# A two-layer encoder trunk on one core: norm factor and offset behind the transpose, with edits to the first k, the scores, the loads and the gate half

## The chip, the core and the metric

The kernel runs on one core of a Trainium2 chip. A core has a matmul engine (PE, with its weight loads, PEld), a vector engine (DVE), a scalar engine (ACT), GpSimd (POOL) and a sync engine (SP) that issues the DMAs. Each engine works through its own queue in order. SBUF is the memory on the core, with 128 partitions; PSUM is where PE writes, in 8 banks of 128 x 512 fp32 values. The metric is the device time of one execution in microseconds (us). A profiled execution also has a span: the time from its first to its last instruction.

## The reference

The input is 256 frames of width 2048, in fp32. Two layers follow each other, and each has a token mixer and a gated MLP, both closed by a layer norm over the residual:

```python
for i in range(DEPTH):                       # DEPTH = 2
    if i % 2 == 0:
        m = gmlp_mixer(x, gm_w_in, gm_ln_g, gm_ln_b, gm_w_s, gm_b_s, gm_w_out)
    else:
        m = mla_mixer(x, mla_w_in, ...)
    x = layer_norm(ALPHA * x + m, ln_mix_g[i], ln_mix_b[i])
    f = conv_ffn(x, ffn_w_up[i], ffn_conv_w[i], ffn_conv_b[i], ffn_w_down[i])
    x = layer_norm(ALPHA * x + f, ln_ffn_g[i], ln_ffn_b[i])
```

- The gMLP mixer computes gelu(x @ w_in), 2048 to 2 x 6144, and splits it into u and v (v is the gate half). v gets a layer norm and a masked 128 x 128 mixing over positions, multiplies u, and goes through w_out, 6144 to 2048.
- The MLA mixer is latent attention: low-rank latents of 512 for queries and for keys with values, 16 heads, a rotary part of 64, a chunk-causal mask.
- conv_ffn is an up projection to 2 x 5504, a causal width-3 convolution over positions, silu(g) * a, and a down projection.
- layer_norm subtracts the mean, divides by the root of the variance plus 1e-5, multiplies by a factor g and adds an offset b, both 2048 wide.

## The kernel before

**Products in three parts.** Each fp32 operand is split into a high part, rounded to the fp32r format of PE, and the rest: ACT casts the high part, DVE subtracts it. A product is then high x high, low x high and high x low, three matmuls. The activations live as xhl tiles with high and low side by side. The weights are streamed from HBM in chunks of 128 x 2048 values (1 MB) by the class Feed: `_load` (L75) issues the DMA on SP, `_split` (L89) does the cast and the subtraction, and `next` (L137) gives a stage its chunk and runs two splits and two loads ahead, more at the end of a down projection.

**Seven instead of eight.** For some pairs of k (two 128-row slices of the weights, two blocks of 128 frames, two 512-wide columns, thus eight products), the kernel takes Strassen's form with seven (`seven`, L344). Such a chunk needs sums of the weights (`_seven`, L113: four more tiles and the adds on DVE) and four combinations of the activations (`combine`, L204), and its partial results go into four more PSUM banks (OWN) beside the usual four (DIRECT); `rest` (L354) puts them together. V_SEVEN says which pairs of the gate half do so in each of its six groups, BACK_SEVEN which k of the down projections.

**The stages in order.** v: six groups of eight chunks, 1024 columns each; `stats` (L567) collects the sums for v's norm. u: twelve groups of 512 columns, each followed by `gate` (L628). Then the down projection `down` (L392) in two halves of 1024 columns, the norm, and the MLP: 22 groups of up projection with `pair` (L682) and again `down`. Layer 1 is the attention (latents, queries, keys, values, scores, output) and the same MLP.

**The class Norm.** `piece` (L527) adds a result to the residual and takes statistics; `start` (L535) makes mean and reciprocal root; `scale` (L541) normalises 128 x 512 values of the residual in place; `put` (L549) transposes them on PE into a PSUM bank and splits them into the xhl tile of the next stage. `prep` (L514) loads factor and offset rows, broadcast over the partitions, towards the end of the down projection. `boundary` (L453) interleaves all that by hand with the last matmuls of the down projection and the first group of the next stage: three chunks of the last columns are kept back (SKEW), so that PE has work while the first 128 frames are normalised.

**First k.** `Sums.quad` (L373) splits four k's of the down projection's input at once into a tile of the pool "big"; `Sums.make` (L383) builds the combinations of a seven.

**Order and buffers.** A planner turns the program into one queue for each engine. It takes the instruction that stands first in the program among those it expects to be ready, so an instruction may move ahead of others that wait. Tiles of one tag share buffers: "big" has 22 of 128 x 2048 fp32 values, for weight chunks, residual, xhl, stage results and the norms' rows alike; "t1" and "t2" are small work tiles, 8 and 6 of them. A tile waits until a buffer of its tag is free.

Of the kernel before, what the change touches and what calls it, by code (L numbers as in the profile page):

```python
# [15 lines left out]
P = 128  # L16
# [32 lines left out]
V_PAIRS = [[0, 1, 2, 3, 4, 5, 6, 7]] + [[2, 0, 1, 4, 3, 5, 6, 7]] * 5  # L49
V_SEVEN = [()] + [(2, 3)] * 5  # L50
# [15 lines left out]
class Feed:  # L66
# [8 lines left out]
    def _load(self):  # L75
# [13 lines left out]
    def _split(self):  # L89
# [9 lines left out]
        step = 512 if i == 0 else cols if kind == "wide" else 1024 if cols == 2048 else cols // 2  # L99
# [45 lines left out]
def trunk(ctx: ExitStack, tc: tile.TileContext, x, xT, gm_in, gm_wout, ffn_up, ffn_dn,  # L145
# [56 lines left out]
    xc, xraw, xc_room = {}, [], [slot([P, 2, 8 * P], "xc0", F32R)]  # L202
# [163 lines left out]
    class Sums:  # L366
# [3 lines left out]
        def __init__(self, src, tag):  # L370
            self.src, self.tag, self.rooms, self.got, self.quads = src, tag, [], {}, {}

        def quad(self, q, n_k):  # L373
# [7 lines left out]
            self.quads[q] = t  # L381

# [9 lines left out]
    def down(n_k, src, tag, ln, sums, skew=SKEW):  # L392
# [5 lines left out]
        for hf, units in enumerate(halves(n_k)):  # L398
# [5 lines left out]
            for i, u in enumerate(units):  # L404
# [8 lines left out]
                a = [[x_parts(quads, k, b) for k in u] for b in range(2)]  # L413
# [84 lines left out]
    class Norm:  # L498
# [15 lines left out]
        def prep(self):  # L514
# [4 lines left out]
            nc.sync.dma_start(self.b, ln_rows[2 * i + 1 : 2 * i + 2, :].to_broadcast([P, D]))  # L519

# [20 lines left out]
        def scale(self, b, f):  # L541
            c = slice(f * 512, (f + 1) * 512)
            r = self.res[b][:, c]
            nc.vector.scalar_tensor_tensor(r, r, self.mu, self.g[:, c], ALU.subtract, ALU.mult)
            nc.vector.scalar_tensor_tensor(r, r, self.rs, self.b[:, c], ALU.mult, ALU.add)
            if self.last:
                nc.sync.dma_start(out[b * P : (b + 1) * P, c], r)

        def put(self, b, f):  # L549
# [7 lines left out]
            t3 = t.rearrange("p (j c) -> p j c", j=4)  # L557
            hi = self.new[f][:, :, b * P : (b + 1) * P]
            nc.scalar.copy(hi, t3)
            nc.vector.tensor_tensor(self.new[f][:, :, S + b * P : S + (b + 1) * P], t3, hi.bitcast(F32), ALU.subtract)  # L560
# [4 lines left out]
    vst = st.tile([P, 2, 12, 6], F32, tag="vst", name="vst", bufs=1)  # L565

    def stats(gi):  # L567
        for b in range(2):
            for f in range(2):
                nc.vector.bn_stats(vst[:, b, 2 * gi + f, :], v[gi][:, b, f * 512 : (f + 1) * 512])  # L570
# [525 lines left out]
```

## Time and profile before

| | us |
|---|---|
| median of 3 runs | 2514.16 |
| lowest and highest run | 2513.23, 2514.31 |
| profiled execution, its own time | 2514.31 |
| its span, first to last instruction | 2512.5 |
| PE busy | 2488.9 (99%) |
| DVE busy | 1833.0 (73%) |
| ACT busy | 1317.0 (52%) |

A row of the profile names line, engine, operation, and the tiles written and read (out<-in). Where a helper issues an instruction, the line is the helper's: all matmuls stand at L162. Waits are listed as waiter, releaser, us in total, times, longest. A stretch row has length, busy time and count of each engine, the granted share of the PE clock, the mean share of the DMA engines and GB/s. In a timeline row the first two numbers are start and duration in us; the bracket tells how long the engine had been idle and what ended that.

### The profile page before, as it was taken

Reading aid. Unit: us, or ns where it says so; the run is one execution under the profiler, and the core shown is the slowest. Engines: PE = TensorE matmul, PEld = TensorE weight load, DVE = VectorE, ACT = ScalarE, POOL = GpSimd, SP = SyncE. Lnnn points to the kernel's source line nnn. Section 1 sums busy time; section 2 is a strip of 40 time slices with the busy share of each in tenths; the row PEclk is TensorE's granted clock in tenths of the full one; section 3 lists DMA queues with packets and bytes.
Section 4 is the critical chain, followed back from the end, with each engine's and each line's share of the span. In section 5 each row is a group of like instructions: output and inputs, shape, how many; then the busy total and the mean of one; then the engine's idle time right before and its main releaser. Section 6 shows DMA issues by size and latency. Waiting matters only on the chain.

```text
span 2512.5 us, 32375 instructions
## 1 busy us (share of the span) xinstructions
PE 2488.9 (99%) x13081; PEld 2140.5 (85%) x13081; DVE 1833.0 (73%) x2411; ACT 1317.0 (52%) x1689; POOL 2.9 (0%) x17
## 2 busy tenths in 40 slices
PE   9999999999999999999999999999999999999998
PEld 7888888888887888888888888988888888888886
DVE  7877766678787767666777897766686677668797
ACT  5555544445464545554655564565365455546553
POOL 0000000000000000000000000000000000000000
PEclk9999999999999999999999999999999999999999
DMA  7555544556566545555546674444454455544654
GB/s 292 201 184 211 191 170 166 177 192 206 189 207 252 190 179 201 184 184 181 189 151 201 217 268 159 152 150 178 177 214 176 167 197 186 183 168 169 212 206 167
DMA packets 86021, 480.18 MB, mean 191 GB/s; under 512 B 7664, under 2 KB 8304, under 8 KB 46064
## 3 DMA queue, kind: packets, MB, share of 16 engines
q1 hardware_dynamic: 85872, 478.13, 53.4%
q8 instruction: 102, 1.67, 0.3%
q14 instruction: 47, 0.39, 0.0%
HBM read 476.00 MB, written 2.10 MB: 190 GB/s over the span
## 4 chain that ended last, share of the span: by engine, by line
PE 96%; DVE 2%; ACT 1%; DMA 1%; issue 0%; SPq 0%; DVEq 0%; ACTq 0%
PE up L162 35%; PE u L162 10%; PE dn_q L162 9%; PE dn_p L162 6%; PE v_q L162 5%; PE wo_q L162 5%; PE mo L162 3%; PE dn_e L162 3%; PE wo_p L162 3%; PE v_p L162 3%; PE v_e L162 2%; PE wo_e L162 2%; PE upf L162 2%; PE mkv L162 1%; PE qn L162 1%; PE kn L162 1%
## 5 line engine op out<-in xcount | busy, mean ns | idle before, releaser
L103 DVE TENSOR_TENSOR wl<-raw,wh 128x1024 fp32r<-128x1024 f32 (+3 forms) x667 | 940.9, 1434 | 226.4 <-ACT wh L102 166.8
L102 ACT CAST wh<-raw 128x1024 fp32r<-128x1024 f32 (+3 forms) x667 | 796.1, 1223 | 364.7 <-DVE wl L103 125.3
L162 PE MATMUL up<-xhl,wh 128*128 128x512 f32 x2624 | 610.7, 390 | 0.0
L162 PEld LDWEIGHTS up<-xhl,wh 128*128 128x128 f32 x2624 | 487.4, 188 | 97.8
L162 PEld LDWEIGHTS up<-xhl,wl 128*128 128x128 f32 x2624 | 325.8, 192 | 6.4
L162 PE MATMUL up<-xhl,wl 128*128 128x256 f32 x2624 | 328.1, 283 | 0.0
L162 PE MATMUL u<-xhl,wh 128*128 128x512 f32 x768 | 183.3, 392 | 0.6 <-DVE h_u L309 0.5
L162 PEld LDWEIGHTS u<-xhl,wh 128*128 128x128 f32 x768 | 141.5, 188 | 30.5 <-PE s L162 2.2
L110 ACT CAST th<-ts 128x1536 fp32r<-128x1536 f32 x80 | 83.2, 1053 | 93.5 <-DVE ts L117 80.7
L111 DVE TENSOR_TENSOR tl<-ts,th 128x1536 fp32r<-128x1536 f32 x80 | 95.0, 1219 | 4.9 <-ACT th L110 2.6
L162 PEld LDWEIGHTS u<-xhl,wl 128*128 128x128 f32 x768 | 95.3, 192 | 1.9
L162 PE MATMUL u<-xhl,wl 128*128 128x256 f32 x768 | 95.9, 283 | 0.0
L162 PE MATMUL v_q<-wh,xhl 128*128 128x512 f32 x304 | 94.0, 391 | 1.3 <-ACT wh L102 1.3
L162 PE MATMUL wo_q<-wh,woa 128*128 128x512 f32 x304 | 94.0, 390 | 0.0
L110 ACT CAST wh<-raw 128x1536 fp32r<-128x1536 f32 x40 | 59.3, 1482 | 50.1 <-DMA raw<-in_ffn_dn_dram 19.6
L162 PE MATMUL dn_q<-wh,dn1a 128*128 128x512 f32 x264 | 82.5, 392 | 2.0 <-DVE dn1a L380 2.0
L162 PE MATMUL dn_q<-wh,dn0a 128*128 128x512 f32 x264 | 82.0, 390 | 2.0 <-DVE dn0a L380 2.0
L162 PE MATMUL mo<-wh,oT 128*128 128x512 f32 x256 | 82.9, 404 | 0.0
L309 DVE TENSOR_TENSOR h_1a<-up,lo_1a 128x256 f32<-128x256 f32 x41 | 17.2, 420 | 75.4 <-ACT lo_1a L307 75.3
L309 DVE TENSOR_TENSOR h_0a<-up,lo_0a 128x256 f32<-128x256 f32 x41 | 17.2, 420 | 74.8 <-ACT lo_0a L307 74.6
L111 DVE TENSOR_TENSOR wl<-raw,wh 128x1536 fp32r<-128x1536 f32 x40 | 70.1, 1751 | 2.1 <-PE dn_q L162 2.1
L162 PEld LDWEIGHTS v_q<-wh,xhl 128*128 128x128 f32 x304 | 56.9, 188 | 13.8 <-ACT wh L102 2.0
(440 smaller groups left out, 3805.8 us busy)
## 6 DMA issues: line engine op xcount, KB each, us to landing
raw<-in_ffn_up_dram SPq DMA_DIRECT2D x172, 1024.0 KB, 4.7
raw<-in_gm_in_dram SPq DMA_DIRECT2D x95, 1024.0 KB, 4.8
raw<-in_ffn_dn_dram SPq DMA_DIRECT2D x84, 1024.0 KB, 5.3
raw<-in_gm_wout_dram SPq DMA_DIRECT2D x48, 1024.0 KB, 5.5
raw<-in_ml_out_dram SPq DMA_DIRECT2D x16, 1024.0 KB, 4.8
raw<-in_ml_b_dram SPq DMA_DIRECT2D x14, 1024.0 KB, 4.8
raw<-in_ml_kv_dram SPq DMA_DIRECT2D x5, 864.0 KB, 4.6
lng<-in_ln_rows_dram SPq DMA_DIRECT2D x4, 1024.0 KB, 7.9
```

The lines of the kernel that those rows point to most:

```text
L102: self.nc.scalar.copy(hi[:, c], raw[:, c])
L103: self.nc.vector.tensor_tensor(lo[:, c], raw[:, c], hi[:, c].bitcast(F32), ALU.subtract)
L110: self.nc.scalar.copy(hi, raw)
L111: self.nc.vector.tensor_tensor(lo, raw, hi.bitcast(F32), ALU.subtract)
L162: nc.tensor.matmul(o, l, r, start=start, stop=stop, skip_group_check=True)
L309: nc.vector.tensor_tensor(h, acc[:, 0:S], lo, ALU.add)
```

## The change

- **Norms.** In all norms but the last, `scale` only subtracts the mean and multiplies by the reciprocal root. `put` applies factor and offset behind the transpose, where they are one value for each partition: four ACT instructions of 128 x 128 with a column of `lncol` as scale and another as bias, into a work tile, which is then split. `lncol` holds all norms' factors and offsets as columns: the rows are loaded once as 128 x 128 values and transposed once on PE. The residual itself gets factor and offset in the next stage, by `restore`, from broadcast rows that are loaded there.
- **First k.** The first four k's of a down projection are split one by one into "t2" tiles (`first`); two combinations instead of four are made in the stage before, the others in the down projection.
- **Scores.** Three `attend_a` and two `attend_b` stand one step earlier between the products of the values.
- **Loads.** Chunks 1 and 2 are loaded and split in halves; the constants and the rotary tables are loaded behind the first group of v.
- **Gate half.** Three of eight chunks in five groups are made by seven products, where there were two, in another order and with another order of banks; v's sums come from the accumulators of ACT (gelu for the sum, a Square for the squares about a first mean), and DVE adds the partial results straight from PSUM.

```diff
-V_PAIRS = [[0, 1, 2, 3, 4, 5, 6, 7]] + [[2, 0, 1, 4, 3, 5, 6, 7]] * 5
-V_SEVEN = [()] + [(2, 3)] * 5
+V_PAIRS = [[0, 1, 2, 3, 4, 5, 6, 7]] + [[0, 2, 1, 5, 3, 6, 4, 7]] * 5
+V_SEVEN = [()] + [(2, 3, 4)] * 5
...
         else:
+            if self.loaded in (1, 2):
+                step = 1024
             for o in range(0, cols, step):
...
-        step = 512 if i == 0 else cols if kind == "wide" else 1024 if cols == 2048 else cols // 2
+        step = 512 if i == 0 else cols if kind == "wide" and i > 2 else 1024 if cols == 2048 else cols // 2
...
-    xc, xraw, xc_room = {}, [], [slot([P, 2, 8 * P], "xc0", F32R)]
+    xc, xraw, xc_room = {}, [], [slot([P, 2, 8 * P], f"xc{i}", F32R) for i in range(2)]
...
-    nc.sync.dma_start(cst, consts)
...
-    nc.sync.dma_start(rope_sb, ropes)
+    lncol = cpool.tile([P, P], F32, name="lncol")
...
+        def first(self):
+            for k in range(4):
+                x = self.src[0][:, k, :]
+                t = tp.tile([P, 512], F32R, tag="t2", name=f"{self.tag}f{k}", bufs=6)
+                nc.scalar.copy(t[:, 0:S], x)
+                nc.vector.tensor_tensor(t[:, S : 2 * S], x, t[:, 0:S].bitcast(F32), ALU.subtract)
+                self.parts[k] = t
+            self.quads[0] = None
...
-        def prep(self):
+        def rows(self):
             i = self.idx
             self.g = slot([P, D], f"lng{i}")
...
+        def prep(self):
+            if self.last:
+                self.rows()
+
+        def restore(self, b, f):
+            c = slice(f * 512, (f + 1) * 512)
+            r = self.res[b][:, c]
+            nc.vector.tensor_tensor(r, r, self.g[:, c], ALU.mult)
+            nc.vector.tensor_tensor(r, r, self.b[:, c], ALU.add)
...
             r = self.res[b][:, c]
+            if not self.last:
+                nc.vector.tensor_scalar(r, r, self.mu, self.rs, op0=ALU.subtract, op1=ALU.mult)
+                return
             nc.vector.scalar_tensor_tensor(r, r, self.mu, self.g[:, c], ALU.subtract, ALU.mult)
             nc.vector.scalar_tensor_tensor(r, r, self.rs, self.b[:, c], ALU.mult, ALU.add)
...
-            t3 = t.rearrange("p (j c) -> p j c", j=4)
+            y = tp.tile([P, 4, P], F32, tag="t2", name=f"lny{i}_{b}_{f}", bufs=6)
+            for j in range(4):
+                g, o = 32 * i + 4 * f + j, 32 * i + 16 + 4 * f + j
+                nc.scalar.activation(y[:, j], t[:, j * P : (j + 1) * P], AF.Identity, bias=lncol[:, o : o + 1],
+                                     scale=lncol[:, g : g + 1])
             hi = self.new[f][:, :, b * P : (b + 1) * P]
-            nc.scalar.copy(hi, t3)
-            nc.vector.tensor_tensor(self.new[f][:, :, S + b * P : S + (b + 1) * P], t3, hi.bitcast(F32), ALU.subtract)
+            nc.scalar.copy(hi, y)
+            nc.vector.tensor_tensor(self.new[f][:, :, S + b * P : S + (b + 1) * P], y, hi.bitcast(F32), ALU.subtract)
...
     def stats(gi):
+        if gi == 0:
+            nc.vector.tensor_scalar(vc, vsum[:, :, 0], -1.0 / 512, None, op0=ALU.mult)
         for b in range(2):
             for f in range(2):
-                nc.vector.bn_stats(vst[:, b, 2 * gi + f, :], v[gi][:, b, f * 512 : (f + 1) * 512])
+                sq = tp.tile([P, 512], F32, tag="t2", name=f"vsq{gi}{b}{f}", bufs=6)
+                nc.scalar.activation(sq, v[gi][:, b, f * 512 : (f + 1) * 512], AF.Square, bias=vc[:, b : b + 1],
+                                     accum_out=vsq[:, b, 2 * gi + f : 2 * gi + f + 1])
...
-        acc = Banks(f"v{gi}", OWN + DIRECT if V_SEVEN[gi] else DIRECT)
+        acc = Banks(f"v{gi}", DIRECT if gi == 0 else DIRECT + OWN if gi % 2 else OWN + DIRECT)
...
-            if c == 0 and gi > 0:
+            if c == 2 and gi > 0:
                 stats(gi - 1)
...
-            if t is None:
-                nc.scalar.activation(o, acc.acc[n], AF.Gelu_apprx_tanh)
-                continue
-            nc.scalar.copy(o, acc.acc[n])
-            nc.vector.tensor_tensor(o, o, t, ALU.add)
-            nc.scalar.activation(o, o, AF.Gelu_apprx_tanh)
+            if t is not None:
+                nc.vector.tensor_tensor(o, acc.acc[n], t, ALU.add)
+            nc.scalar.activation(o, acc.acc[n] if t is None else o, AF.Gelu_apprx_tanh,
+                                 accum_out=vsum[:, i // 2, 2 * gi + i % 2 : 2 * gi + i % 2 + 1])
         v.append(vt)
+        if gi == 0:
+            nc.sync.dma_start(cst, consts)
+            nc.sync.dma_start(rope_sb, ropes)
+            lnrow = tp.tile([P, P], F32, tag="t1", name="lnrow", bufs=8)
+            nc.sync.dma_start(lnrow, ln_rows.rearrange("r (k p) -> (r k) p", p=P))
...
+    lnt = bank("lnrowT")
+    nc.tensor.transpose(lnt[:, 0:P], lnrow, ident)
+    nc.scalar.copy(lncol, lnt[:, 0:P])
...
         if gi == 11:
-            sums.quad(0, NF_GM)
+            sums.first()
         for f in range(4):
             gate(4 * gi + f, acc[f])
-        if gi in (9, 10):
-            for k in BACK_SEVEN[2 * gi - 18 : 2 * gi - 16]:
+        if gi == 10:
+            for k in BACK_SEVEN[:2]:
                 sums.make(k)
...
             if gi == 21:
-                sums.quad(0, NF_FF)
+                sums.first()
...
-            if gi in (19, 20):
-                for k in BACK_SEVEN[2 * gi - 38 : 2 * gi - 36]:
+            if gi == 1:
+                ln.rows()
+            if 3 <= gi < 11:
+                ln.restore((gi - 3) // 4, (gi - 3) % 4)
+            if gi == 20:
+                for k in BACK_SEVEN[:2]:
                     sums.make(k)
...
         if c == 0:
             after_q(1, 1, None)
+            ln.rows()
+        if c >= 2:
+            for f in (2 * (c % 2), 2 * (c % 2) + 1):
+                ln.restore(c // 2 - 1, f)
...
-                if (hf, k) in ((0, 2), (1, 0), (1, 2)):
+                if (hf, k) in ((0, 1), (0, 3), (1, 1)):
                     attend_a(len(probs))
-                if (hf, k) in ((1, 1), (1, 3)):
+                if (hf, k) in ((1, 0), (1, 2)):
                     attend_b(k // 2)
```

More of the change, by code (lines that the diff above doesn't have):

```diff
@@ L371, in __init__ @@
             self.src, self.tag, self.rooms, self.got, self.quads = src, tag, [], {}, {}
+            self.parts = {}
+        def first(self):
[6 more added lines that the diff above has]
+            self.quads[0] = None
         def quad(self, q, n_k):
@@ L381, in quad @@
             self.quads[q] = t
+            for k in range(4 * q, 4 * q + n):
+                self.parts[k] = t[:, k % 4, :]
         def make(self, k):
@@ L412, in down @@
                     ln.prep()
-                a = [[x_parts(quads, k, b) for k in u] for b in range(2)]
+                a = [[(sums.parts[k][:, b * P : (b + 1) * P], sums.parts[k][:, S + b * P : S + (b + 1) * P])
+                      for k in u] for b in range(2)]
                 if left < skew:
```

16 lines of the change are left out of this document (11 added, 5 removed).

## The prediction

> **What bounds the kernel now.** I read the page first, then the matmul engine's own waits, then the timeline around each of them, and last the busy time of stretches.
>
> ```profile
> span 2512.5 us, 32375 instructions
> PE 2488.9 (99%) x13081; PEld 2140.5 (85%) x13081; DVE 1833.0 (73%) x2411; ACT 1317.0 (52%) x1689; POOL 2.9 (0%) x17
> PE 96%; DVE 2%; ACT 1%; DMA 1%; issue 0%; SPq 0%; DVEq 0%; ACTq 0%
> ```
>
> PE is busy for 99% of the span and makes 96% of the chain that ended last. So time goes only where PE has less to do, or where one of its few waits goes. These are nearly all of them (the warm-up's own 1.3 us is left out; columns: waiter, releaser, us in total, times, longest):
>
> ```profile
> PE upf L162 <- DVE xhl L560: 2.2, 1, 2.2
> PE dn_q L162 <- DVE dn0a L380: 2.0, 1, 2.0
> PE dn_q L162 <- DVE dn1a L380: 2.0, 1, 2.0
> PE mq L162 <- DVE xhl L560: 1.5, 1, 1.5
> ...
> PE v_q L162 <- ACT wh L102: 1.3, 1, 1.3
> PE v_p L162 <- ACT wh L102: 1.1, 2, 0.7
> PE pt L918 <- DVE p L910: 0.8, 1, 0.8
> PE u L162 <- DVE h_u L309: 0.5, 1, 0.5
> PE v_q L162 <- DVE wl L103: 0.2, 1, 0.2
> ```
>
> They sum to 11.6 us. Two cost more than they show. The next rows are stretches: length; PE, weight loads, DVE, ACT, POOL busy; granted PE clock; DMA share and rate.
>
> ```profile
> 136.00:178.00 42.00, 42.00 (x187) 34.79 (x186) 33.41 (x31) 22.48 (x22) 0.00 (x0) 1.00 0.57 201
> 845.00:1295.00 450.00, 450.00 (x2596) 398.61 (x2595) 307.51 (x472) 246.78 (x371) 0.00 (x0) 1.00 0.52 184
> 1553.00:1579.00 26.00, 26.00 (x198) 26.00 (x197) 16.13 (x22) 14.06 (x26) 0.00 (x0) 1.00 0.66 251
> 812.00:818.00 6.00, 5.18 (x18) 4.14 (x19) 4.54 (x8) 0.33 (x1) 0.00 (x0) 0.72 0.34 142
> 2273.00:2279.00 6.00, 4.98 (x15) 3.98 (x16) 6.00 (x11) 3.42 (x6) 0.00 (x0) 0.72 0.00 0
> 1298.70:1302.00 3.30, 3.29 (x15) 2.74 (x15) 3.30 (x7) 1.64 (x4) 0.32 (x2) 1.00 0.00 0
> 2502.00:2512.50 10.50, 0.14 (x1) 0.00 (x0) 7.09 (x12) 0.29 (x1) 0.00 (x0) 0.70 0.26 100
> ```
>
> Behind the 2.2 us wait and behind the 2.0 us wait of layer 1 (rows 812.00 and 2273.00) the clock averages 0.72 over 6 us: 0.28 x 6 = 1.7 us lost each. Behind the equal wait of layer 0 (row 1298.70) it stays 1.00. So the waits are worth 11.6 + 3.4 = 15.0 us. The last row is the tail after the last matmul, some 10.4 us, and the last norm keeps its old path: nothing changes there.
>
> **First k (sums.first, L655 and L717; sums.make, L659 and L721).** At the start of layer 0's down projection:
>
> ```profile
> 1283.84 0.37 ACT L307 COPY lo_0a<-up 128x256 f32<-128x256 f32 x1 [9.99 <-PE up L162]
> ```
> ```profile
> 1294.40 1.99 ACT L379 CAST dn0a<-act 128x1024 fp32r<-128x1024 f32 x2
> ```
> ```profile
> 1297.44 1.22 DVE L380 TENSOR_TENSOR dn0a<-act,dn0a 128x1024 fp32r<-128x1024 f32 x1
> ```
>
> The quad of four k's is cast only at 1294.4, though ACT had idled 10 us until 1283.8 and its source was written long before; what it lacked, as I read it, was one of the 22 "big" buffers. DVE then needs until 1298.7, and PE waits. The change takes four small "t2" tiles, a tag that the up stage hardly uses, so the same work (4 casts, 4 subtractions) fits into that idle time. It also makes two combinations ahead instead of four, one "big" buffer less. Both waits and one slow clock go: 2.0 + 2.0 + 1.7 = 5.7 us. What is late next is the second chunk's lo half, needed only after 24 matmuls, 5.4 us at 0.225 us each (42.00 us / 187 in the first row of the stretches): covered. The three combinations made later run one unit (5 us) ahead; the fifth of the before was made like that without a wait. The gmlp's down projection has no wait to lose. Bounds: 0 if the planner leaves them behind the casts (no loss, as the first k alone needs a quarter of the quad's work), and 5.7; I take 5.7.
>
> **Norms (Norm.scale, put, restore, rows).** Around the 2.2 us wait, three DVE rows, then ACT, then PE:
>
> ```profile
> 803.64 2.35 DVE L103 TENSOR_TENSOR wl<-raw,wh 128x1024 fp32r<-128x1024 f32 x2
> ...
> 809.83 2.34 DVE L103 TENSOR_TENSOR wl<-raw,wh 128x1024 fp32r<-128x1024 f32 x2
> 812.09 1.28 DVE L560 TENSOR_TENSOR xhl<-lnt,xhl 128x512 fp32r<-128x512 f32 x2
> ```
> ```profile
> 808.13 0.59 ACT L559 CAST xhl<-lnt 128x512 fp32r<-128x512 f32 x1 [2.96 <-PE lnt L556]
> ```
> ```profile
> 810.13 0.48 PE L162 MATMUL upf<-wh,xhl 128*128 128x512 f32 x1
> ```
>
> The lo half could have started at 808.7, when ACT was done. It started at 812.1, since DVE's in-order queue held norm arithmetic and two weight splits (2.3 us each) ahead of it. The prices (min/median/max ns):
>
> ```profile
> L544 DVE SCALAR_TENSOR_TENSOR res<-res,lnmv,lng x32: 730/745/753, 803.0 to 2507.3; 128x512 f32<-128x512 f32 x32
> L620 DVE TENSOR_SCALAR v<-v,vmv,vrs x12: 793/804/806, 270.5 to 278.5; 128x1024 f32<-128x1024 f32 x12
> L775 ACT ACTIVATE cq<-ct,cst x8: 367/368/371, 1549.3 to 1563.1; 128x128 fp32r<-128x128 f32 x8
> L570 DVE BATCH_NORM_STATS2 vst<-v x24: 673/684/695, 51.7 to 266.6; 128x6 f32<-128x512 f32 x24
> ```
>
> scale falls from two such instructions (2 x 0.745; L545 is of the same shape and kind) to one TENSOR_SCALAR, for which half of the 1024-wide one, 0.40, and all of it, 0.80, are the bounds; I take 0.45. DVE is relieved of 1.0 us per piece. put gains four 128x128 ACTIVATEs with factor and offset columns: 4 x 0.37 = 1.5 us, about 1.1 where they overlap; ACT's 0.59 copy follows as before. How long they took between the aggregate and PE's need, L544 first (stretch, length, DVE busy):
>
> ```profile
> 802.90:810.10 7.20, 2.22 (x3) 1.00 0.37 142
> ```
> ```profile
> 802.90:810.10 7.20, 1.41 (x2) 1.00 0.37 142
> ```
>
> The 3.6 us become three scales, 1.4: 2.3 us less, about the wait itself. The way through ACT, even behind the first 2.35 us split, is reciprocal to 806.1, scale 806.6, transposes 807.2, ACT 808.9 (1.1 + 0.6), subtraction 809.6: before the need. The two weight splits may move too, since factor and offset no longer hold two "big" buffers there. The other wait (mq, 1.5 us) has the same form. Removed: 2.2 + 1.7 + 1.5 = 5.4; with 0.4 kept back for the longer ACT chain I take 5.0. Ends: the waits stay and grow by 1.1 each (-2.2), and 5.4. The third boundary, behind the attention, has no wait.
>
> restore adds two 128x512 DVE instructions (of L544's size, 0.75) eight times in three stages, 12 us each. In the up stage they lie in groups 3 to 10, where DVE is busy 307.5 of 450 us: hidden; without that cover they would cost 36 us. In the MLA they lie beside the key/value chunks (1553 to 1579), where DVE has 9.9 us free of 26 and the query chunks after it have more: tight, 0 to 3 us, I take 0, because PE runs two split chunks ahead. The two row loads move on SP from the end of each down projection behind the first chunks of the next stage; there DMA is busy 0.52 (up) and 0.66. In the MLA a late landing would hold restore, and with it the weight splits queued behind it on DVE.
>
> **Gate half (V_SEVEN, stats, v's evacuation).** A chunk by seven products takes 7 x 3 matmuls instead of 24. One more chunk in five groups: 15 matmuls x 0.225 = 3.4 us that PE no longer spends. DVE pays the split:
>
> ```profile
> L111 DVE TENSOR_TENSOR wl<-raw,wh x40: 1747/1751/1758, 39.9 to 2449.0; 128x1536 fp32r<-128x1536 f32 x40
> ```
>
> That is 1.22 (1024 wide, as L380's) + 1.75 twice + 0.68 three times (512 wide, as L570's) = 6.8, against 2.35 for a plain chunk: +4.4, and the four bn_stats (2.7) leave. 33.4 + 1.7 = 35.1 of 41.3 us per group. ACT loses four copies and gains four Squares, the accumulator reads and 1.7 us of casts: 22.5 to about 26. Both stay below PE. The new order puts plain chunks between the sevens. Buffers are the doubt: an extra room and five tiles per seven, with v's tiles filling the pool. Bounds 3.4 and -2; I take 3.4. v's banks are now freed by DVE's add (0.69) and not by ACT's copy (0.59); the plain chunk that opens a group needs one each 1.4 us (6 matmuls): 0, and C below where DVE is late. The sums at the end are a dozen 128x1 instructions beside the first u matmuls: 0.
>
> **Loads (Feed._load and _split, consts).** Chunk 1:
>
> ```profile
> 11.55 1.90 ACT L102 CAST wh<-raw 128x2048 fp32r<-128x2048 f32 x1 [2.48 <-DMA raw<-in_gm_in_dram]
> ...
> 16.45 1.91 ACT L102 CAST wh<-raw 128x2048 fp32r<-128x2048 f32 x1 [1.96 <-DMA raw<-in_gm_in_dram]
> 18.89 1.92 ACT L102 CAST wh<-raw 128x2048 fp32r<-128x2048 f32 x1 [0.53 <-DMA raw<-in_gm_in_dram]
> ```
>
> A chunk lands in 2.44 us (16.45 to 18.89), so half of it 1.2 us earlier, at 10.3; its half cast (1.0) ends at 11.4, while PE is busy until 12.2. The waits of 1.3 and 0.2 go: 1.5. Two more issues on SP are paid by the two that leave (cst, rope). If the planner still issues cst that early (128 x 792 values, 0.4 MB, 1 us at this rate), chunk 2 is that much later; bounds 0.5 and 2. The 1.1 of chunk 0 stays.
>
> **Scores.** The wait on p is that of head 3, whose place the diff doesn't move; I take 0 of 0.8. The u wait: 0 of 0.5. One transpose and a copy for lncol: -0.1.
>
> **The sum.** 5.7 + 5.0 + 3.4 + 1.5 - 0.1 = 15.5 us off the profiled execution: span 2512.5 to 2497.0, its own time 2514.3 to 2498.8. It stands 0.15 us above the median, so 2514.2 - 15.5 = 2498.7.
>
> [...] Rows 812.00 and 2273.00 show the clock halved for a while behind waits of 2.2 and 2.0 us, row 1298.70 not behind 2.0. [...]
>
> **The rivals.**
> (B) The boundary waits stay, as ACT's longer chain takes DVE's place: the 5.0 goes, 2.2 more is lost: 2505.9. For: ACT's 1.1 to 1.5 us more per piece exceed DVE's 1.0 less, and 2.0 us casts queue between the puts. [...] Against: ACT is busy 0.33 of 6 us behind 812, and the queue that PE waits for is DVE's.
> (C) The gate half waits for buffers or DVE, about 1.4 us per group: 7 us back, 2505.7. For: 35 of 41 us. Against: no wait there before.
> (D) Slower: PE consumes one put per 12 matmuls, 2.7 us. put now takes ACT 1.7, and with a 2.0 cast between two puts 3.7, so 1.0 too much: four pieces in three boundaries 12 us, with the clock halved each time 5.1 more, and the 5.0 not won: 2498.7 + 22.1 = 2520.8. It decides where every chunk of a boundary is cast there rather than ahead; before, the puts came with idle ACT in front (2.96 us at 808.13).
> (E) The planner leaves the first-k copies where the quad was: 5.7 stays, 2504.4.
> (F) The two slow clock stretches don't come from the waits and stay: 2498.7 + 3.4 = 2502.1. For: row 1298.70. Against: both begin right behind a wait, and no other row here is slow before the tail.
>
> **How the numbers follow.** Forecast 2498.7: 0.56; B 0.16; C 0.12; E 0.06; F 0.03; D 0.07. 0.2% (5 us, 2509.1 to 2519.2) is about what a measurement can tell from no change. Faster: forecast, B, E, F and most of C, 0.88; same, C with more than planned, 0.05; slower, D, 0.07. Low end: the scores' 0.8, u's 0.5, the kept-back 0.4, 0.5 more of loads and chunk 0's 1.1 are won too, 2495.4, and the runs before spread over 1.1 us: 2494. High end: B with half of C, 2509. The forecast's own range is 2494 to 2503.
>
> **What would show it.** No row of PE waiting on dn0a or dn1a, and 128x256 casts ahead of 1290; clock 1.00 through both boundaries; 15 matmuls of 128x512 fewer in the gate half; chunk 1's first matmul near 12.2. Wrong, if a new wait of PE stands in the gate half, on a put's ACTIVATE, or on a weight split behind restore.

## The result, and the profile after

The changed kernel takes 2505.5 us (median of 7 runs, 2504.8 to 2507.0) beside 2513.2 us (median of 7, 2512.0 to 2514.4) for the kernel before on the same chip. The ratio is 0.9969, with a 95% interval of 0.9958 to 0.9981: 7.7 us faster, where 15.5 had been forecast. The profiled execution took 2505.5 us itself, with a span of 2503.7, which is 8.8 less than the span before.

From the page of the changed kernel, the span, the busy times and the chain that ended last:

```profile
span 2503.7 us, 32617 instructions
PE 2484.9 (99%) x13067; PEld 2137.1 (85%) x13067; DVE 1847.7 (74%) x2463; ACT 1369.3 (55%) x1860; POOL 2.9 (0%) x17
PE 98%; DVE 1%; ACT 0%; DMA 0%; SPq 0%; issue 0%; DVEq 0%; ACTq 0%
```

PE has 14 matmuls fewer: 15 of the third seven, and one transpose more. PE's waits in the changed kernel (waiter, releaser, us in total, times, longest), all of them:

```profile
PE kn L164 <- DVE qnT L929: 2.4, 1, 2.4
PE krt L875 <- ACT kr L868: 1.4, 1, 1.4
PE warm L164 <- POOL idle L199: 1.3, 1, 1.3
PE v_q L164 <- ACT wh L104: 1.0, 2, 0.7
PE pt L979 <- DVE p L971: 0.8, 1, 0.8
PE mq L164 <- DVE xhl L592: 0.4, 1, 0.4
PE v_p L164 <- ACT wh L104: 0.3, 1, 0.3
PE u L164 <- DVE h_u L310: 0.2, 1, 0.2
PE mq L164 <- ACT xhl L591: 0.2, 1, 0.2
```

The three waits of 2.0 to 2.2 us that led the list before are gone, and so are the slow clocks behind two of them. The two rows at the top are new. Both stand in the latents of layer 1, the stage in which `restore` was put beside the key/value chunks. Stretches of the changed kernel (length; PE, weight loads, DVE, ACT, POOL busy; granted clock; DMA share and rate): a group of the gate half, the first boundary, the start of layer 0's and of layer 1's down projection, the key/value chunks, and the place of the 2.4 us wait with the 3.3 us behind it:

```profile
130.00:172.00 42.00, 42.00 (x187) 34.79 (x186) 37.48 (x34) 26.91 (x33) 0.00 (x0) 1.00 0.57 201
800.00:812.00 12.00, 12.00 (x63) 9.98 (x61) 9.86 (x17) 8.10 (x21) 0.00 (x0) 1.00 0.48 175
1286.00:1292.00 6.00, 6.00 (x28) 4.99 (x27) 6.00 (x8) 3.80 (x7) 0.16 (x1) 1.00 0.36 102
2262.00:2270.00 8.00, 8.00 (x39) 6.69 (x38) 8.00 (x13) 5.79 (x7) 0.00 (x0) 1.00 0.43 150
1550.00:1566.50 16.50, 16.50 (x126) 16.50 (x125) 13.95 (x20) 5.95 (x9) 0.00 (x0) 1.00 0.74 271
1604.80:1608.20 3.40, 0.98 (x9) 0.78 (x8) 3.40 (x7) 3.40 (x7) 0.00 (x0) 1.00 0.56 176
1608.30:1611.60 3.30, 3.30 (x18) 3.30 (x17) 3.30 (x6) 3.25 (x7) 0.00 (x0) 0.50 0.30 127
```

In the first four PE is busy all the time at clock 1.00: what the change was to do there, it does. In the last row the clock is halved for 3.3 us, so about 1.7 us are lost on top of the waits of 2.4 and 1.4: some 5.5 us in the latents.

How the latents get there shows in the timeline of the changed kernel. First ACT, then DVE, then PE (start, duration; the bracket is the idle time before and what ended it):

```profile
1555.03 2.00 ACT L104 CAST wh<-raw 128x1024 fp32r<-128x1024 f32 x2 [1.09 <-PE mkv L164]
1566.63 0.41 ACT L814 ACTIVATE sq<-mkv 128x288 f32<-128x288 f32 x1 [9.60 <-PE mkv L164]
...
1567.38 3.90 ACT L104 CAST wh<-raw 128x1024 fp32r<-128x1024 f32 x4
```
```profile
1568.45 1.22 DVE L105 TENSOR_TENSOR wl<-raw,wh 128x1024 fp32r<-128x1024 f32 x1 [3.98 <-ACT wh L104]
...
1603.72 1.23 DVE L906 TENSOR_TENSOR qrs<-qr,qrs 128x1024 f32<-128x1024 f32 x1 [1.11 <-ACT qrs L905]
1604.86 2.36 DVE L105 TENSOR_TENSOR wl<-raw,wh 128x1024 fp32r<-128x1024 f32 x2
1607.13 1.41 DVE L929 TENSOR_TENSOR qnT<-qn,qnT 128x256 fp32r<-128x256 f32 x4
```
```profile
1581.74 0.33 PE L875 MATMUL krt<-ident,kr 128*128 128x128 f32 x1 [1.39 <-ACT kr L868]
1607.61 0.51 PE L164 MATMUL kn<-ckv,wh 128*128 128x256 f32 x2 [2.42 <-DVE qnT L929]
```

ACT casts two halves of weight chunks and then stands idle for 9.6 us in front of the key latent's squares, which need the last key/value product. Four more casts come only behind the squares. DVE, which has splits to make, runs dry for 3.98 us and gets four splits at once when the key latent, its rotary part and the query heads are due as well. Five of `restore`'s sixteen instructions, too, run only now, between these splits (1569.6 to 1573.8), so that DVE starts to scale the key latent at 1576.1. It does not catch up: the subtractions that PE waits for (as I read it, they free the banks for the first key head) begin at 1607.1, and PE, ready at 1605.2, starts at 1607.6.

### The profile page after: what moved, and what is told of

The parts are those of the page before. It is cut to its first block, busy times and chain, and to the rows that moved or that the text cites. A ratio compares the mean times of both kernels' runs of the same rounds, so it can differ in the third digit from the quotient of the medians.

```text
span 2503.7 us, 32617 instructions
## 1 busy us (share of the span) xinstructions
PE 2484.9 (99%) x13067; PEld 2137.1 (85%) x13067; DVE 1847.7 (74%) x2463; ACT 1369.3 (55%) x1860; POOL 2.9 (0%) x17
## 4 chain that ended last, share of the span: by engine, by line
PE 98%; DVE 1%; ACT 0%; DMA 0%; SPq 0%; issue 0%; DVEq 0%; ACTq 0%
PE up L164 36%; PE u L164 11%; PE dn_q L164 9%; PE dn_p L164 6%; PE wo_q L164 5%; PE v_q L164 5%; PE dn_e L164 4%; PE mo L164 3%; PE v_p L164 3%; PE wo_p L164 3%; PE wo_e L164 2%; PE upf L164 2%; PE v_e L164 2%; PE mkv L164 1%; PE kn L164 1%; PE qn L164 1%
## 5 line engine op out<-in xcount | busy, mean ns | idle before, releaser
L105 DVE TENSOR_TENSOR wl<-raw,wh 128x1024 fp32r<-128x1024 f32 (+3 forms) x664 | 929.8, 1424 | 211.0 <-ACT wh L104 157.5
L104 ACT CAST wh<-raw 128x1024 fp32r<-128x1024 f32 (+3 forms) x664 | 786.4, 1215 | 331.5 <-DVE wl L105 120.4
L112 ACT CAST th<-ts 128x1536 fp32r<-128x1536 f32 x90 | 93.0, 1052 | 114.6 <-DVE ts L119 85.2
L113 DVE TENSOR_TENSOR tl<-ts,th 128x1536 fp32r<-128x1536 f32 x90 | 106.5, 1219 | 11.3 <-ACT th L112 10.5
L112 ACT CAST wh<-raw 128x1536 fp32r<-128x1536 f32 x45 | 66.7, 1483 | 46.3 <-DMA raw<-in_ffn_dn_dram 11.5
L113 DVE TENSOR_TENSOR wl<-raw,wh 128x1536 fp32r<-128x1536 f32 x45 | 78.8, 1752 | 6.5 <-PE dn_q L164 3.0
L164 PE MATMUL v_q<-wh,xhl 128*128 128x512 f32 x264 | 81.7, 390 | 1.0 <-ACT wh L104 1.0
L164 PE MATMUL dn_q<-wh,dn1a 128*128 128x512 f32 x248 | 76.4, 389 | 0.0
L164 PE MATMUL dn_q<-wh,dn0a 128*128 128x512 f32 x248 | 76.3, 389 | 0.0
L164 PEld LDWEIGHTS wo_q<-wh,woa 128*128 128x128 f32 x288 | 54.1, 188 | 11.2
```

The lines of the kernel that those rows point to most:

```text
L104: self.nc.scalar.copy(hi[:, c], raw[:, c])
L105: self.nc.vector.tensor_tensor(lo[:, c], raw[:, c], hi[:, c].bitcast(F32), ALU.subtract)
L112: self.nc.scalar.copy(hi, raw)
L113: self.nc.vector.tensor_tensor(lo, raw, hi.bitcast(F32), ALU.subtract)
L164: nc.tensor.matmul(o, l, r, start=start, stop=stop, skip_group_check=True)
```

## The experiments

All runs are compared with the kernel before on the same chip: a median of 2514.0 us for the first two groups of four, 2513.9 for the last. "Gain" is the difference to that median, beside the changed kernel's 7.7.

| run | us | ratio to before, 95% interval | gain |
|---|---|---|---|
| e1_restore_late | 2500.6 | 0.9950 [0.9937, 0.9962] | 13.4 |
| e2_token_restore | 2500.5 | 0.9950 [0.9937, 0.9962] | 13.5 |
| e3_no_rows | 2500.1 | 0.9948 [0.9935, 0.9960] | 13.9 |
| e5_old_norm1 | 2499.3 | 0.9946 [0.9933, 0.9960] | 14.7 |
| e10_work_here | 2499.3 | 0.9946 [0.9932, 0.9960] | 14.7 |
| e7_quad | 2512.2 | 0.9996 [0.9987, 1.0004] | 1.8 |
| e6_gate_two | 2509.7 | 0.9984 [0.9975, 0.9993] | 4.4 |
| e4_old_norms | 2502.7 | 0.9958 [0.9946, 0.9971] | 11.4 |
| e13_held | 2499.6 | 0.9944 [0.9932, 0.9957] | 14.3 |
| e17_rows_one_later | 2503.2 | 0.9961 [0.9949, 0.9974] | 10.7 |
| e11_rows_early | 2500.0 | 0.9946 [0.9933, 0.9958] | 13.9 |
| e12_heads | 2500.0 | 0.9947 [0.9933, 0.9960] | 13.9 |

The changed kernel was timed only beside its own group, so a difference of two gains sets groups on different chips against each other, and each interval reaches 2 to 3 us to either side. Differences of some 3 us between two gains are therefore read together with the traces.

**Restore out of the latents.** The row loads and pieces move into the loop over the attention heads.

```diff
-            ln.rows()
-        if c >= 2:
-            for f in (2 * (c % 2), 2 * (c % 2) + 1):
-                ln.restore(c // 2 - 1, f)
...
-    ln = Norm(2, res)
+    lnp, ln = ln, Norm(2, res)
...
+        if t == 4:
+            lnp.rows()
+        if 6 <= t < 14:
+            lnp.restore((t - 6) // 4, (t - 6) % 4)
```

> The changed kernel, with the restore of layer 0's last norm moved out of the latents: its two row loads and its sixteen DVE instructions now stand in the loop over the attention heads (loads at head 4, one piece per head 6 to 13). Theory W (restore's DVE work delays the key latent, the rotary part and the query splits): the waits of 1.4 and 2.4 us and the slow clock behind the second (1.7) go, so about 2505.5 - 5.6 = 2499.9. Theory L (the two 1 MB loads and the two buffers they hold make the weight chunks of the latent stage late): the same, 2499.9. Theory O (the waits come from the order of the other edits, not from restore): 2505.5, the waits stay. A new wait in the attention is possible, where DVE is busy 40.5 of 60 us.

Measured 2500.6: both waits and the slow clock are gone, so theory O falls. The waits on the scores' p grew from 0.8 to 2.1 us, where restore now lies.

**Work without loads, loads without work.** Two runs were to tell W from L.

```diff
-        def restore(self, b, f):
-            c = slice(f * 512, (f + 1) * 512)
+        def restore(self, b, f, n=512):
+            c = slice(f * 512, f * 512 + n)
...
-                ln.restore(c // 2 - 1, f)
+                ln.restore(c // 2 - 1, f, 1)
```

> The changed kernel, with both row loads kept in the latents, but each of the sixteen restore instructions there only one column wide instead of 512 (the rest of that residual gets no factor and offset, which leaves work out). Theory W (DVE work): DVE is relieved of 16 x (0.68 - 0.15) = 8.5 us and the waits go, 2499.9. Theory L (loads and buffers): the waits stay, 2505.5. Theory O (order of other edits): 2505.5.

```diff
-            nc.vector.tensor_tensor(r, r, self.g[:, c], ALU.mult)
-            nc.vector.tensor_tensor(r, r, self.b[:, c], ALU.add)
+            g, o = (self.g[:, c], self.b[:, c]) if self.g is not None else (cst[:, 0:512], cst[:, 0:512])
+            nc.vector.tensor_tensor(r, r, g, ALU.mult)
+            nc.vector.tensor_tensor(r, r, o, ALU.add)
...
-            ln.rows()
+            ln.g = ln.b = None
```

> The changed kernel, with restore's sixteen DVE instructions kept in the latents at full width, but without the two row loads and their two buffers: they read a tile of constants that is on the core anyway (other values in place of factor and offset). Theory W (DVE work): the waits stay, 2505.5. Theory L (loads and buffers): the waits go, 2499.9. Theory O (order of other edits): 2505.5.

Measured 2500.5 and 2500.1. Taking away either one is enough, which neither theory allows. The token run keeps a wait of 1.0 us on kn, so loads alone leave a part. The run without rows turned out not to be clean: with nothing to wait for, its restore had slipped forward beside the boundary. The first and the last of its sixteen rows on DVE:

```profile
1519.42 1.28 DVE L545 TENSOR_TENSOR res<-res,cst 128x512 f32<-128x512 f32 x2
...
1538.99 0.69 DVE L546 TENSOR_TENSOR res<-res,cst 128x512 f32<-128x512 f32 x1
```

**Work at its place, and buffers at theirs.** So the next run ties restore to a value that is finished at 1550, and a later one also holds the two buffers, filled by GpSimd.

```diff
...
-            ln.rows()
+            ln.g = ln.b = cq[0][:, 3, :].bitcast(F32)
```

> The changed kernel without the two row loads in the latents, but with restore's sixteen full-width DVE instructions kept at the time where the changed kernel has them: they read the last finished piece of the query latent (in place of factor and offset, which leaves these out), so they can't start before 1550 us. The run without row loads had let them slip to 1519 to 1540, beside the boundary. Theory W (DVE work at that place is enough): the waits of 1.4 and 2.4 us and the slow clock stay, 2505.5. Theory L (loads and buffers alone): 2500.1, as without rows. Theory B (only both together, work that holds the splits and chunks that come late): also about 2500, with at most 1 us of waits in the heads.

```diff
...
-            ln.rows()
+            ln.g, ln.b = slot([P, D], "lng"), slot([P, D], "lnb")
+            nc.gpsimd.memset(ln.g, 1.0)
+            nc.gpsimd.memset(ln.b, 0.0)
+            ln.m = cq[0][:, 3, :].bitcast(F32)
```

> The changed kernel with restore's sixteen full-width DVE instructions in the latents and with the two row tiles held there as before, but filled by GpSimd instead of by loads (ones and zeros; the first instruction of each pair reads the last finished piece of the query latent, so that it can't start before 1550; factor and offset are left out). In the queues that the planner wrote, three weight chunks are cast ahead of the key latent's squares, as in the kernel before, where the changed kernel has one. Theory Q (the waits go with the number of chunks cast ahead of the squares: none at three, 1.0 us at two, 3.8 and a slow clock at one): no wait in the heads, about 2500. Theory H (buffers held together with work on DVE make the splits late on the chip, whatever the order): the waits of 1.4 and 2.4 stay, 2505.5.

Measured 2499.3 and 2499.6. The key/value chunks of the run with the buffers held (first row) and of the one without (second), and ACT's casts ahead of the squares in the latter:

```profile
1550.00:1566.50 16.50, 16.50 (x126) 16.50 (x125) 16.47 (x24) 9.70 (x13) 0.00 (x0) 1.00 0.79 293
```
```profile
1550.00:1566.50 16.50, 16.50 (x126) 16.50 (x125) 16.45 (x23) 9.70 (x12) 0.00 (x0) 1.00 0.71 265
```
```profile
1551.50 6.20 ACT L104 CAST wh<-raw 128x864 fp32r<-128x864 f32 x8
1558.50 2.00 ACT L104 CAST wh<-raw 128x1024 fp32r<-128x1024 f32 x2 [0.80 <-DMA raw<-in_ml_b_dram]
1566.58 0.41 ACT L815 ACTIVATE sq<-mkv 128x288 f32<-128x288 f32 x1 [6.08 <-PE mkv L164]
```

DVE is busy 16.45 of 16.5 us here, 2.5 more than in the changed kernel (13.95), and the latents have only 0.2 us of waits. The eight casts of the first ACT row are four of the key/value chunks and four halves of weight chunks, with two more in the second: six halves stand ahead of the squares, where the changed kernel has two. Six it was in the kernel before, too:

```profile
1563.34 3.89 ACT L102 CAST wh<-raw 128x1024 fp32r<-128x1024 f32 x4
1567.92 2.00 ACT L102 CAST wh<-raw 128x1024 fp32r<-128x1024 f32 x2 [0.69 <-PE mkv L162]
1577.90 0.41 ACT L757 ACTIVATE sq<-mkv 128x288 f32<-128x288 f32 x1 [7.98 <-PE mkv L162]
```

So DVE could carry restore; theories W and H fall. Theory L fell with the token run, but for its wait of 1.0 us, and what is left is theory B: only the work and the loads together cost the time. What differs in these traces is how much of the other work stands ahead of the squares in ACT's queue.

**The same work, loads and buffers one chunk later.** This run was to test the order alone; only the row loads move, and the pieces stay.

```diff
         if c == 0:
             after_q(1, 1, None)
-            ln.rows()
+        if c == 1:
+            ln.rows()
...
```

> The changed kernel with the same restore, the same row loads and the same two buffers in the same stage: the loads stand one key/value chunk later (behind the second instead of the first) and the pieces two per chunk from the third on. The planner's queue then has two weight chunks cast ahead of the key latent's squares instead of one. Theory Q (order of the casts): a wait of about 1.0 us in the heads and no slow clock, as in the run with the token restore, 2505.5 - 5.6 + 1.0 = 2500.9. Theory H (work, loads and buffers in this stage): 2505.5.

Measured 2503.2, between the two forecasts, with these waits:

```profile
PE kn L164 <- DVE qnT L930: 2.4, 1, 2.4
...
PE krt L876 <- ACT kr L869: 1.0, 1, 1.0
```

Four halves are ahead of the squares here, as in the token run, yet the kn wait is 2.4 and not 1.0: theory Q, which counts the casts, doesn't hold as it stands. Nor are the latents much better off than in the changed kernel. Of the 2.9 us between the two profiled executions only 0.4 is waits in the latents; 0.9 is waits at the start of v (1.3 to 0.4), and behind the 2.4 us wait the matmuls kept their pace this time (two of 128x256 in 0.40 us at 1607.14, where the changed kernel has 0.63 at 1608.76), which saves the 1.7 of the slow clock.

The traces show another queue at work. By 1572.3 DVE had scaled the first block of the key latent here, by 1572.1 in the run with the buffers held. PE transposes it at 1572.7 there, but at 1575.4 here, and has no idle time before it: in PE's queue the transposes stand behind other matmuls. PE of the held run, then PE, ACT and DVE of this run:

```profile
1572.73 0.60 PE L829 MATMUL ct<-ident,hqk 128*128 128x128 f32 x4
```
```profile
1575.42 0.38 PE L828 MATMUL ct<-ident,hqk 128*128 128x128 f32 x2
```
```profile
1576.36 0.37 ACT L832 ACTIVATE ckv<-ct,cst 128x128 fp32r<-128x128 f32 x1 [6.14 <-PE ct L828]
```
```profile
1576.76 0.35 DVE L833 SCALAR_TENSOR_TENSOR ckv<-ct,cst,ckv 128x128 fp32r<-128x128 f32 x1 [3.79 <-ACT ckv L832]
```

So DVE again idles for almost 4 us, as ACT stands in front of an instruction that waits for PE, while the casts of the rotary key, ready at 1572.9, stand behind that instruction. The place is another one than in the changed kernel, the pattern is the same. What goes with the waits in all these runs is when DVE is done with the rotary part of the queries, the work in front of the subtraction that PE waits for. The rows of its two last subtractions on DVE in the changed kernel, this run, and the one with the buffers held (min/median/max ns, first and last start):

```profile
L906 DVE TENSOR_TENSOR qrs<-qr,qrs x2: 1220/1224/1227, 1595.1 to 1603.7; 128x1024 f32<-128x1024 f32 x2
```
```profile
L907 DVE TENSOR_TENSOR qrs<-qr,qrs x2: 1224/1224/1225, 1593.7 to 1602.3; 128x1024 f32<-128x1024 f32 x2
```
```profile
L910 DVE TENSOR_TENSOR qrs<-qr,qrs x2: 1224/1225/1226, 1590.4 to 1599.1; 128x1024 f32<-128x1024 f32 x2
```

With the token run and the one tied to 1550, the last starts are 1603.7 (changed), 1602.3 (this run), 1600.3 (token), 1599.4 (tied) and 1599.1 (held); in the same order the waits in the latents together (krt and kn) are 3.8, 3.4, 1.0, 0.2 and 0.2.

**The parts undone, one by one.** First k:

```diff
-            sums.first()
+            sums.quad(0, NF_GM)
...
-        if gi == 10:
-            for k in BACK_SEVEN[:2]:
+        if gi in (9, 10):
+            for k in BACK_SEVEN[2 * gi - 18 : 2 * gi - 16]:
...
-                sums.first()
+                sums.quad(0, NF_FF)
...
```

> The changed kernel with the first four k's of each down projection split at once as before (one big tile, four combinations in the stage ahead). By the prediction's sum: both waits of 2.0 us on the second half come back, and one slow clock of 1.7, so 2505.5 + 5.7 = 2511.2. If other edits (norms, loads) had freed the buffer in time: 2505.5, and the first k gained nothing by itself.

The gain falls to 1.8, by 5.9. Both waits are back (waits of this run):

```profile
PE dn_q L164 <- DVE dn1a L392: 2.0, 1, 2.0
PE dn_q L164 <- DVE dn0a L392: 2.0, 1, 2.0
```

The third seven:

```diff
-V_PAIRS = [[0, 1, 2, 3, 4, 5, 6, 7]] + [[0, 2, 1, 5, 3, 6, 4, 7]] * 5
-V_SEVEN = [()] + [(2, 3, 4)] * 5
+V_PAIRS = [[0, 1, 2, 3, 4, 5, 6, 7]] + [[0, 2, 1, 3, 4, 5, 6, 7]] * 5
+V_SEVEN = [()] + [(2, 3)] * 5
```

> The changed kernel with two instead of three chunks by seven products in each of five groups of the gate half (same order of pairs else, same statistics). By the prediction's sum: 15 matmuls of 128x512 more, 15 x 0.225 = 3.4 us, so 2508.9. If the third seven is partly given back by waits or by the later stages: less, down to 2505.5.

The gain falls to 4.4, by 3.3. The intervals of the two gains overlap (1.8 to 6.3 us here, 4.8 to 10.6 for the changed kernel); the traces have the 15 matmuls between them (13082 and 13067).

All norms as before:

```diff
...
-            if not self.last:
-                nc.vector.tensor_scalar(r, r, self.mu, self.rs, op0=ALU.subtract, op1=ALU.mult)
-                return
...
-            y = tp.tile([P, 4, P], F32, tag="t2", name=f"lny{i}_{b}_{f}", bufs=6)
...
+            y = t.rearrange("p (j c) -> p j c", j=4)
...
-            if 3 <= gi < 11:
-                ln.restore((gi - 3) // 4, (gi - 3) % 4)
...
```

> The changed kernel with all norms as before: factor and offset in two DVE instructions per piece ahead of the transpose, rows loaded at the end of the down projections, no restore anywhere. The prediction's term for the norms is 5.0 (boundary waits of 2.2 and 1.5 and one slow clock); against it stand about 5.6 behind restore in the latents. So if both are right the norms part is worth nothing as a whole: 2505.5 - 5.6 + 5.0 = 2504.9. If the boundary gain is not due to the norms part: 2499.9.

The gain rises to 11.4: as built, the norms part made the kernel 3.7 us slower (2.8 by the medians themselves). Its gain at the boundaries is seen beside the next run, which keeps the new norms but at one place:

```diff
-            if self.last:
+            if self.last or self.idx == 1:
                 self.rows()
...
-            if not self.last:
+            if not self.last and self.idx != 1:
...
+            y = t.rearrange("p (j c) -> p j c", j=4)
-            y = tp.tile([P, 4, P], F32, tag="t2", name=f"lny{i}_{b}_{f}", bufs=6)
-            for j in range(4):
+            if i != 1:
+                y = tp.tile([P, 4, P], F32, tag="t2", name=f"lny{i}_{b}_{f}", bufs=6)
+            for j in range(4 if i != 1 else 0):
...
```

> The changed kernel, with the norm ahead of the latents alone as before (factor and offset in two DVE instructions per piece in front of the transpose, rows loaded in the down projection, no restore). Theories W and L: the 5.6 us behind restore go, and the wait at the boundary into the latents comes back from 0.6 to 1.5 us, so 2505.5 - 5.6 + 0.9 = 2500.8. Theory O: 2505.5 + 0.9 = 2506.4.

Measured 2499.3. Between these two runs stand 3.3 us, the worth of the new norms at the two other boundaries; between the profiled executions it is 2.4, of which 2.2 is the wait of the first boundary. The waits of the run with all norms as before still have the row of the first boundary, and the wait into the latents:

```profile
PE upf L164 <- DVE xhl L585: 2.2, 1, 2.2
PE mq L164 <- DVE xhl L585: 1.5, 1, 1.5
```

**Other places for restore.** The rows of that norm loaded at the end of the down projection, or rows and pieces moved into the key heads:

```diff
-            if self.last:
+            if self.last or self.idx == 1:
                 self.rows()
...
         if c == 0:
             after_q(1, 1, None)
-            ln.rows()
```

> The changed kernel with the rows of the norm ahead of the latents loaded at the end of the down projection, as before the change, and restore left where it stands in the program: with the rows there, its pieces can run as soon as a piece is scaled, beside the boundary (1519 to 1540). Three chunks are cast ahead of the squares. Both theories: no wait in the heads; the boundary keeps 0.6 us: about 2499.9. If restore delays the boundary's pieces on DVE: up to 1 us more there.

```diff
...
+        if i == 0:
+            ln.rows()
         heads(kT, ckv, i, "kn")
+        if i >= 2:
+            for f in range(4):
+                ln.restore(i - 2, f)
```

> The changed kernel with the MLA's row loads and restore moved to the key heads (loads ahead of the first, pieces behind the third and fourth), where PE has no wait and DVE is busy 21 of 32 us. Three chunks are cast ahead of the squares. Expected: no wait in the latents, 2499.9; if the splits of the value chunks fall behind restore, a wait at the start of the values, up to 2 us.

Both measured 2500.0, as forecast; with the rows early, PE's wait at the boundary grew from 0.6 to 1.1 us. With 2499.3 to 2500.6, e5, e11, e12 and e1, which leave nothing of the reference out, lie below both kernels, some 5 to 6 us below the changed one; their intervals do not tell them apart. Among them e5 has the old norm ahead of the latents, with its 1.5 us wait, so that the new norm gains anything at that boundary isn't shown.

Not undone by themselves: the loads and the scores. What is said of them below is read from the traces.

## Why the prediction was half right

The forecast was 2498.7, the result 2505.5: inside the range of 2494 to 2509, but outside the forecast's own range of 2494 to 2503. That it lies in the wide range is luck: its upper end was added up from rivals B and C, which didn't come, and the loss that did come stands in none of the rivals. In the runs that take restore out of the latents and leave nothing out, the gain is 13.4 to 14.7 of the forecast 15.5. By its steps:

- **First k, 5.7: right.** Undone, it costs 5.9. That a missing "big" buffer was the reason stays a reading, as that run undoes the tiles and the number of combinations together. The casts of layer 0 ran long ahead of need, not just ahead of 1290 (min/median/max ns, first and last start in the changed kernel):

```profile
L380 ACT CAST dn0f<-act x4: 401/405/411, 960.3 to 964.9; 128x256 fp32r<-128x256 f32 x4
```

- **Gate half, 3.4: right.** Undone, it costs 3.3. Over five groups (50.0 to 256.5) DVE was busy 34.0 us a group and ACT 25.3, where 35.1 and about 26 had been worked out; the stretch shown above is fuller, with 37.48 and 26.91 of 42. PE stayed at 42.00. Rival C did not come.
- **Norms at the boundaries, 5.0: right in kind, too large.** The prices held: a `scale` of 0.54 us (0.45 taken), four ACTIVATEs of `put` 1.50 (1.1 to 1.5 taken). The lo half that PE needs began at 803.65, 2.2 us behind the start of the ACTIVATEs, and PE didn't wait. The group of all scales in the changed kernel (min/median/max ns), then its first `put` in the timelines of ACT and DVE:

```profile
L571 DVE TENSOR_SCALAR res<-res,lnmv,lnrs x24: 529/542/548, 799.0 to 1788.6; 128x512 f32<-128x512 f32 x24
```
```profile
801.46 1.50 ACT L588 ACTIVATE lny<-lnt,lncol 128x128 f32<-128x128 f32 x4 [0.81 <-PE lnt L584]
803.00 0.62 ACT L591 CAST xhl<-lny 128x512 fp32r<-128x512 f32 x1
```
```profile
803.65 0.69 DVE L592 TENSOR_TENSOR xhl<-lny,xhl 128x512 fp32r<-128x512 f32 x1 [0.79 <-ACT xhl L591]
```

  The 2.2 us wait went in full. Of the 1.5 us into the latents 0.6 stayed: 0.4 on DVE's subtraction and 0.2 on ACT (the row `mq <- ACT xhl` is new), whose longer way rival B had named. And the slow clock was counted at a full 1.7, though it comes only in some runs (below). What was measured is 3.3, without the boundary into the latents.
- **restore in the MLA, "tight, 0 to 3 us, I take 0, because PE runs two split chunks ahead": the step that failed.** It cost about 5.5 to 6 us (3.8 of waits and 1.7 of clock; 5.7 by moving restore away). The sum of DVE's free time was right: the runs with DVE at 16.45 of 16.5 show that it could have carried the work. What the step left out is that the two chunks ahead are themselves made by ACT and DVE in queues that are written in advance. With the row loads and the pieces at that place, four casts ended behind the squares, DVE idled 4 us with work pending, and the cover was gone when the key latent needed DVE. The prediction's sentence on a late landing that "would hold restore, and with it the weight splits queued behind it" had the right place and the wrong queue: the splits were held by ACT's casts, behind another instruction, and on DVE a late split held restore. None of the rivals had this wait; the nearest sign was "on a weight split behind restore", among those that would make the prediction wrong.
- **Loads, 1.5: about right.** The waits of v at the start fell from 2.6 to 1.3 us. With the same loads the other runs have 0.4 to 1.5 us of waits there, so the term can't be told more sharply. The load of the constants, which the change puts behind the first group of v, still went out at 6.89 us (5.96 before), a case that the prediction had named. The first matmul of chunk 1 started at 12.23 behind 0.29 us:

```profile
12.23 0.73 PE L164 MATMUL v_q<-wh,xhl 128*128 128x512 f32 x2 [0.29 <-ACT wh L104]
```

- **Scores, 0 of 0.8: right.** The row on p is 0.8 in both. **u, 0 of 0.5: nearly**, it fell to 0.2.
- **Rival F** (the slow clocks don't come from the waits): its ground was that one equal wait kept the clock at 1.00, but that differs from one execution to the next. The wait on dn0a, at clock 1.00 before, has 0.50 in the run with first k undone; the 2.2 us wait of the first boundary, at 0.72 before, has 1.00 with the norms as before:

```profile
1292.00:1294.20 2.20, 2.20 (x7) 1.71 (x6) 2.20 (x5) 1.76 (x2) 0.16 (x1) 0.50 0.00 0
```
```profile
800.00:812.00 12.00, 9.79 (x49) 7.72 (x49) 11.95 (x18) 2.27 (x4) 0.00 (x0) 1.00 0.50 175
```

**What stays open.** Shown is that the loss needs both the row loads and the full work at that place, that holding buffers and working without the loads costs nothing, and that the queues differ. The trace of the changed kernel speaks against the loads' own time on the DMA queues as the cause. The two chunks of the late casts were issued at 1551.8 and 1556.6 and landed 4.8 us later each, at 1556.6 and 1561.4, while ACT stood idle from 1557.0 to 1566.6 with the squares ahead of the casts. In the token run, with the same row loads, the first of these chunks was issued at 1551.8 too and was cast by 1558.9. Not shown is whether buffers for these casts were free before 1566.6, and why the planner wrote the queues so: no run kept the order of the changed kernel and took away only the transfers. The run one chunk later also shows that the number of casts ahead isn't the whole of it.

## What to carry to other kernels

An engine's free time in a stage is not enough to call moved work hidden there: ask what the stage's other queues will look like once its loads and its pieces are in them, above all which instruction that waits for PE could come to stand in front of work that runs ahead. When a fixed piece of work has a wide choice of places (restore may lie anywhere between two norms), put it where no chain of small dependent steps follows: the same sixteen instructions cost about 6 us beside the latents, about half a microsecond of PE's waits in the boundary and none in the key heads or in the up projection. And a stand-in that removes a dependency may move: look in the trace where it ran before its time is read.

## What was not expected of the hardware

A wait of PE of about 2 us does not always halve the clock. Equal waits at equal places had it halved in one execution and not in another: behind the wait on dn0a it is 1.00 before and 0.50 with first k undone, behind the wait of the first boundary it is 0.72 over 6 us before and 1.00 with the norms as before (rival F). The times of the kernel before, which has four waits of 1.5 to 2.2 us, spread with it. Its 21 runs beside the second group (e10, e7, e6, e4), by mean granted clock:

| mean clock | runs | us |
|---|---|---|
| 0.999 | 2 | 2510.6 to 2511.2 |
| 0.998 | 10 | 2512.1 to 2514.2 |
| 0.997 | 9 | 2514.0 to 2514.9 |

The medians of the three rows lie 1.6 and 1.8 us apart, about the 1.7 us that one halving of 3.4 us costs (in the kernel before the clock is 0.51 from 813.2 to 816.6 and 0.50 from 2274.2 to 2277.6). The experiments whose longest wait is 1.5 us or less (e1, e2, e3, e5, e10 to e13) spread over 0.6 to 2.1 us in five runs each, the kernel before over 4.3 in its 21. The spread isn't the clock behind long waits alone: the run with 2.1 (e10) has no wait over 0.8 us behind the warm-up. In the changed kernel the 3.40 us ahead of the halved clock hold 0.98 us of PE's work (row 1604.80). Why the same wait is followed by the halved clock in one execution and not in another isn't shown.
